# The second token group's last down pair as seven-of-eight rounds, mixed into the third group's first gate products, and half of the third group's y in a pool of its own

## The chip, the cores and the metric

The kernel runs on one core of one Trainium2 chip. The metric is the time of one execution in device microseconds (us); lower is better. Before the change it is 1999.62 us, the median of three runs (1998.15 to 1999.84).

## The reference, cut to what matters

The reference is one decoder layer on 2048 prompt tokens and 8 sample tokens (2056 in all), with a width of 1024 and a feed-forward width of 2816, in fp32. The change touches the last stage only:

```python
D_MODEL = 1024
D_FF = -(-8 * D_MODEL // (3 * 256)) * 256          # 2816
...
h = x + jnp.einsum('bte,ed->btd', mix, w_out)
hn = _rmsnorm(h, norm2_g)
ff = jax.nn.silu(jnp.einsum('btd,df->btf', hn, w_gate)) * jnp.einsum('btd,df->btf', hn, w_up)
y = h + jnp.einsum('btf,fd->btd', ff, w_down)
...
y_prompt = _rmsnorm(yp, final_norm_g)
y_sample = _rmsnorm(ys, final_norm_g)
```

What comes ahead of it (input projection, a gated linear recurrence, sliding-window attention, output projection) is the same work before and after.

## The kernel before, in words

**Products.** An fp32 product is made of three matmuls in fp32r: high part of the weight by high part of the data, high by low, and low by high. A high part is a cast on ACT; the low part is what the cast left over, a subtraction on DVE or POOL.

**Groups, pairs and products.** The feed-forward stage goes over three groups of tokens (`HALVES`: twice 344, twice 342 and twice 342 tokens; I call them the first, second and third group, 0, 1 and 2 in names). Inside a group it goes over 11 pairs (`NPAIR`) of 128-wide blocks of the feed-forward width. The gate and the up product of a pair are seven block products in place of eight each (a Strassen-Winograd scheme; `PRODS` is their order: 1, 2, 6, 5, 7, 3, 4), each of 12 matmuls of 128x342. A matmul is named after its product: g2_0_1 is gate product 1 of the third group's pair 0, u1_10_4 is up product 4 of the second group's pair 10. Their data are the hn tiles (the normed h, with sums and differences of its blocks).

**Down.** The pair's gated product then goes through w_down into y, 16 tiles of 128 x 342 (8 row tiles m, two token halves n) that hold h at first. There are two forms. The direct one (`down`, PSUM tiles pd) takes 16 tiles x 2 blocks x 3 = 96 matmuls and 16 adds into y on DVE. The seven-of-eight form (`down_parts`, PSUM tiles pw) takes 14 rounds of 2 tiles x 3 = 84 matmuls and 28 adds. A round n is product `DPRODS[n % 7]` of half `n // 7`. The data of its seven products are called T: four of them lie in the tiles fh and fl (high and low parts, one buffer for each), three (6, 7 and 4) in the t tiles, t2_0 and t2_1 for the third group. `wino(gi, p)` chooses: before, the direct form is used for pairs 0 to 2 of the first group and for the last pair of every group, the other for the rest. The rounds of pair p are mixed into the products of pair p+1. The direct down of a group's last pair runs behind the first three gate products (`N_EARLY`) of the next group.

**Weights of the rounds.** `down_make` (first group that uses a pair's rounds) loads w_down in pieces (rd), makes their sums on DVE and POOL, splits them into high and low parts (wd: ACT cast L1972, POOL or DVE low part L1973) and stores the sums to a buffer in DRAM, sums_d. `down_load` (later groups) loads the sums from there.

**Rooms.** One pool, bigp, has 16 buffers of three slots each. It holds the hn of the first three products, y (16 slots, 6 buffers for a group) and the t tiles (2 buffers). A new tile takes the room that the order gives it, and its first write waits until the last use of what was there before has ended. y is loaded from DRAM (`y_load`).

**Finish.** When y of a token half is complete, `finish` squares and adds it (DVE and POOL), sums over partitions on PE (st_f), makes the inverse root, transposes it to a row on PE (tr_f), copies the row out (ACT L1149), stores it to DRAM (rows_f, L1150) and loads it again as a tile with the row in every partition (rb_f, L1156), scales the eight y tiles on DVE (L2195) and stores them (out_yT, L2196). f1_1 is the finish of the second group's token half 1. The stores and loads are issued from one queue, SP's.

**Order.** `plan()` gives every product, round and finish a planned time. From these come priorities, and the order of instructions on each engine is written out in a long table, `ORDER`, which is recorded as dependencies: no engine departs from it.

Of the kernel before, what the change touches and what calls it, by code (L numbers as in the profile page):

```python
# [2383 lines left out]
```

## Time and profile before

| | |
|---|---|
| time, median of 3 runs | 1999.62 us (1998.15 to 1999.84) |
| the profiled execution | 1999.11 us, of which the profile's span is 1997.0 |
| mean granted clock of TensorE | 0.997 of full speed |
| PE (matmul) busy | 1971.0 us, 99% of the span |
| PEld (weight load) busy | 1874.8 us, 94% |
| DVE busy | 1560.6 us, 78% |
| ACT busy | 981.3 us, 49% |
| POOL busy | 959.8 us, 48% |
| moved by DMA | 461.93 MB, 231 GB/s over the span |

Busy time is the time in which an engine worked, summed over its instructions. Matmuls overlap their neighbours, so that a busy PE may still lose time by small steps. The second group's last pair and the third group's first pairs run between about 1500 and 1620 us of the span.

### The profile page before, as it was taken

The page shows a single profiled execution, that of the slowest core. Times are in us where ns is not written, and L with a number is a line of the kernel's source. Part 1 is how long each engine was busy: PE and PEld are TensorE (multiplying, and loading weights), DVE is VectorE, ACT ScalarE, POOL GpSimd, SP SyncE. Part 2 cuts the span into 40 slices and gives each one's busy share as a digit, 9 for nine tenths or more (in the row PEclk, how much of TensorE's full clock was granted, in tenths as well). Part 3 has the DMA queues.
Part 4 walks back from the last instruction along what each step waited for, and adds up shares of the span by engine and source line. Part 5 has one row for each costly group of instructions (what it writes and reads, how often), then busy time and mean ns, then how long its engine had stood idle before and what let it go on. Part 6 is the DMA issues. An engine that isn't in the chain of part 4 may idle for free. (4 is left out here: it accounts for less than half of the span.)

```text
span 1997.0 us, 34846 instructions
## 1 busy us (share of the span) xinstructions
PE 1971.0 (99%) x12112; PEld 1874.8 (94%) x12112; DVE 1560.6 (78%) x2894; ACT 981.3 (49%) x2032; POOL 959.8 (48%) x821
## 2 busy tenths in 40 slices
PE   8999999999999999999999999999999999999998
PEld 8988898888877999999999999999999999999998
DVE  7887986777986888888998786886668586766776
ACT  6775774664664534444446433433345433433433
POOL 5412362130233896788998754534456423322323
PEclk9999999999999999999999999999999999999999
DMA  8873586576688978655667886776558675565552
GB/s 314 287 252 138 194 300 198 183 254 210 223 283 291 335 263 268 220 215 210 246 241 279 265 289 231 234 237 210 191 191 267 228 259 199 179 211 195 180 181 103
DMA packets 218470, 461.93 MB, mean 231 GB/s; under 512 B 26230, under 2 KB 90406, under 8 KB 218278
## 3 DMA queue, kind: packets, MB, share of 16 engines
q1 hardware_dynamic: 214662, 456.69, 67.4%
q10 hardware_dynamic: 3632, 3.02, 0.4%
q8 instruction: 95, 1.56, 0.3%
q14 instruction: 81, 0.66, 0.1%
HBM read 345.51 MB, written 115.17 MB: 231 GB/s over the span
## 5 line engine op out<-in xcount | busy, mean ns | idle before, releaser
L1070 PE MATMUL ps_g<-hn,w_g 128*128 128x342 f32 (+1 forms) x2772 | 569.4, 320 | 0.3 <-DMA w_g<-split_g 0.3
L1070 PE MATMUL ps_u<-hn,w_u 128*128 128x342 f32 (+1 forms) x2772 | 559.5, 320 | 1.5 <-DMA w_u<-split_u 0.9
L1070 PEld LDWEIGHTS ps_g<-hn,w_g 128*128 128x128 f32 x2772 | 461.3, 188 | 1.2 <-ACT wd L1972 0.5
L1070 PEld LDWEIGHTS ps_u<-hn,w_u 128*128 128x128 f32 x2772 | 459.5, 188 | 3.0 <-ACT c_u L2115 1.6
L2175 DVE TENSOR_TENSOR y<-y,pw 128x342 f32<-128x342 f32 (+1 forms) x756 | 359.1, 504 | 114.7 <-PE pw L1070 108.4
L1070 PE MATMUL ip<-xn,w_in 128*128 128x512 f32 (+1 forms) x1680 | 365.2, 357 | 6.1 <-ACT xn L1105 5.7
L1070 PEld LDWEIGHTS ip<-xn,w_in 128*128 128x128 f32 x1680 | 269.6, 189 | 45.8 <-ACT xn L1105 5.7
L1070 PE MATMUL pw<-fh,wd 128*128 128x342 f32 (+1 forms) x864 | 253.4, 320 | 0.5 <-DVE y L2175 0.5
L1070 PE MATMUL pw<-t,wd 128*128 128x342 f32 (+1 forms) x972 | 243.7, 320 | 2.8 <-DVE y L2175 2.7
L1070 PE MATMUL op<-mix,w_out 128*128 128x512 f32 (+1 forms) x960 | 205.8, 355 | 0.4 <-ACT mix L1544 0.4
L1070 PEld LDWEIGHTS op<-mix,w_out 128*128 128x128 f32 x960 | 157.5, 189 | 25.3 <-ACT mix L1544 0.8
L1070 PEld LDWEIGHTS pw<-t,wd 128*128 128x128 f32 x972 | 169.9, 188 | 4.9 <-DVE y L2175 4.0
L1973 POOL TENSOR_TENSOR wd<-rd,wd 128x512 fp32r<-128x512 f32 x85 | 121.8, 1434 | 103.4 <-ACT wd L1972 99.1
L1972 ACT CAST wd<-rd 128x512 fp32r<-128x512 f32 x159 | 98.6, 621 | 130.0 <-PE ps_u L1070 39.8
L1070 PEld LDWEIGHTS pw<-fh,wd 128*128 128x128 f32 x864 | 158.6, 188 | 1.2 <-DVE y L2175 0.8
L1904 POOL TENSOR_TENSOR w_u<-ru,w_u 128x512 fp32r<-128x512 f32 x44 | 61.4, 1395 | 170.2 <-ACT w_u L1903 95.9
L1070 PE MATMUL pw<-fl,wd 128*128 128x342 f32 (+1 forms) x432 | 132.9, 320 | 0.0
L2089 DVE TENSOR_TENSOR c_u<-c_u,ps_u 128x342 f32<-128x342 f32 (+1 forms) x99 | 50.2, 508 | 101.2 <-PE ps_u L1070 93.9
L2071 POOL TENSOR_TENSOR c_u<-c_u,c_g 128x342 f32<-128x342 f32 (+1 forms) x60 | 65.4, 1090 | 124.8 <-DVE c_u L2089 115.1
L2060 DVE TENSOR_TENSOR fl<-c_u,fh 128x342 fp32r<-128x342 f32 (+1 forms) x132 | 105.4, 803 | 17.7 <-ACT fh L2059 17.0
L2059 ACT CAST fh<-c_u 128x342 fp32r<-128x342 f32 (+1 forms) x132 | 63.0, 480 | 110.6 <-POOL c_u L2071 49.3
L1070 PE MATMUL pd<-fh,w_d 128*128 128x344 f32 (+1 forms) x384 | 92.9, 320 | 0.0
(319 smaller groups left out, 3490.7 us busy)
## 6 DMA issues: line engine op xcount, KB each, us to landing
w_g<-split_g SPq DMA_DIRECT2D x88, 512.0 KB
w_u<-split_u SPq DMA_DIRECT2D x88, 512.0 KB
w_in<-split_w SPq DMA_DIRECT2D x84, 512.0 KB
rg<-in_wgate SPq DMA_DIRECT2D x110, 256.0 KB
ru<-in_wup SPq DMA_DIRECT2D x110, 256.0 KB
w_out<-split_w SPq DMA_DIRECT2D x48, 512.0 KB
split_g<-w_g SPq DMA_DIRECT2D x44, 512.0 KB
split_u<-w_u SPq DMA_DIRECT2D x44, 512.0 KB
```

The lines of the kernel that those rows point to most:

```text
L1070: r = nc.tensor.matmul(*args, **kw)
L1904: lo_eng.tensor_tensor(w[:, 1, :], src, w[:, 0, :].bitcast(F32), op=ALU.subtract)
L1972: nc.scalar.copy(w[:, :, 0], v)
L1973: eng((E_DLO0, E_DLO1, E_DLO2)[gi][j]).tensor_tensor(w[:, :, 1], v, w[:, :, 0].bitcast(F32), op=ALU.subtract)
L2059: nc.scalar.copy(hi, v)
L2060: nc.vector.tensor_tensor(lo, v, hi.bitcast(F32), ALU.subtract)
L2071: (nc.vector if p == NPAIR - 1 or src is not v else eng(E_MUL[2 * h + n])).tensor_tensor(v, src, g, op=ALU.mult)
L2089: nc.vector.tensor_tensor(o, a, b, op)
L2175: nc.vector.tensor_tensor(v, v, ps, ALU.add)
```

## The change: what it does

The second group's last pair takes the seven-of-eight form, and its 14 rounds stand behind the third group's first gate products. Eight of the 16 y tiles of the third group (row tiles 0, 1, 4 and 5 of both token halves) are loaded into a new pool, yx, that nothing else uses; the other eight stay in bigp, where they now take 3 buffers in place of 6. The sums of a pair's down weights are stored to sums_d only where the next group will load them (`wino(gi + 1, p)`). The order table is written anew for all engines.

```diff
 def wino(gi, p):
-    return p < NPAIR - 1 and (gi > 0 or p >= 3)
+    return gi == 1 or p < NPAIR - 1 and (gi > 0 or p >= 3)
...
-            mixed = p and wino(gi, p - 1)
+            gq, q = (gi, p - 1) if p else (gi - 1, NPAIR - 1)
+            mixed = gq >= 0 and wino(gq, q)
...
-                prod[gi, p, "gu"[i // 7], i % 7] = t - (U_D if gi and not p and i < N_EARLY else 0)
+                prod[gi, p, "gu"[i // 7], i % 7] = t - (U_D if gi and not p and not mixed and i < N_EARLY else 0)
                 t += U_M
-                if mixed and i >= (R_AT if p > 1 else R_FIRST):
+                if mixed and i >= (R_AT if p != 1 else R_FIRST):
                     for n in range(n, min(14, n + 2)):
-                        rounds[gi, p - 1, n] = t
+                        rounds[gq, q, n] = t
                         t += U_R
                     n += 1
+        if wino(gi, p):
+            end.append(t + R_AT * U_M + 7 * (U_M + 2 * U_R))
+            continue
...
+            yx = B(tc.tile_pool(name="yx", bufs=1))
...
-                        y = ys[gi, n, m] = next(place)[:, :nn]
+                        if gi == 2 and m % 4 < 2:
+                            y = yx.tile([P, TP], F32, tag=f"y{n}{m}", name=f"yx_{n}{m}")[:, :nn]
+                        else:
+                            y = next(place)[:, :nn]
+                        ys[gi, n, m] = y
...
-                    if j not in (3, 6):
+                    if j not in (3, 6) and wino(gi + 1, p):
...
                                 nc.vector.tensor_tensor(v, v, ps, ALU.add)
+                        if p == NPAIR - 1 and r in (2, 3, 4, 7):
+                            fire(("y", gi) + {2: (0, m), 3: (1, m), 7: (1, m + 4), 4: (0, m + 4)}[r])
...
     "PE": """
...
-ip0_1_0 ip0_1_1 ip0_1_0 ip0_1_1 ip0_1_0 ip0_1_1 w_st_x0:2 ip0_1_0 w_st_x0:2 ip0_1_1 w_st_x0:3 ip0_12_0:2 ip0_1_0:2
+ip0_1_0 ip0_1_1:2 ip0_1_0:2 ip0_1_1 w_st_x0 ip0_12_1 ip0_12_0 ip0_12_1 w_st_x0 ip0_12_0 ip0_12_1 ip0_12_0 ip0_1_0
```

In numbers of instructions: direct down matmuls 192 before and 96 after, round matmuls 1680 and 1764; DVE adds from pd into y 32 and 16, from pw into y 560 and 588 (140 of them into yx); loads of down weights of 128 KB 134 and 144, of 256 KB 24 and 20.

In the rows below a name ends in a number that the build gives it; what stands ahead of that is group, pair, product and, for pw, the tile (pw1_10_5_1 is product 5, tile 1 of the second group's pair 10). First PE, at the group boundary, behind the last matmuls of u1_10_4. Before:

```order
L1070 MATMUL ps_u1_10_1_17738<-hn1_1_10_13085,w_u1_10_4_17795 128x342
L1070 MATMUL ps_g2_0_2_18028<-hn2_0_3_17849,w_g2_0_2_17853 128x342
L1070 MATMUL ps_g2_0_2_18028<-hn2_0_4_17859,w_g2_0_2_17853 128x342 x4
L1070 MATMUL ps_g2_0_2_18028<-hn2_0_5_17877,w_g2_0_2_17853 128x342
L1070 MATMUL ps_g2_0_1_17995<-hn2_0_6_17891,w_g2_0_6_17889 128x342 x3
L1070 MATMUL ps_g2_0_2_18028<-hn2_0_4_17859,w_g2_0_2_17853 128x342
L1070 MATMUL ps_g2_0_1_17995<-hn2_0_7_17895,w_g2_0_6_17889 128x342
L1070 MATMUL ps_g2_0_1_17995<-hn2_0_6_17891,w_g2_0_6_17889 128x342
L1070 MATMUL ps_g2_0_1_17995<-hn2_0_7_17895,w_g2_0_6_17889 128x342 x2
L1070 MATMUL pd1_10_1_1_18071<-fh1_10_01_7623,w_d1_10_00_17884 128x342
```

And after:

```order
L1079 MATMUL ps_u1_10_1_17807<-hn1_1_10_13088,w_u1_10_4_17906 128x342
L1079 MATMUL ps_g2_0_2_18049<-hn2_0_3_17692,w_g2_0_2_17945 128x342
L1079 MATMUL ps_g2_0_2_18049<-hn2_0_4_17715,w_g2_0_2_17945 128x342 x4
L1079 MATMUL ps_g2_0_2_18049<-hn2_0_5_17719,w_g2_0_2_17945 128x342
L1079 MATMUL ps_g2_0_1_18030<-hn2_0_6_17736,w_g2_0_6_17962 128x342 x3
L1079 MATMUL ps_g2_0_2_18049<-hn2_0_4_17715,w_g2_0_2_17945 128x342
L1079 MATMUL pw1_10_5_1_18103<-fh1_10_01_7626,wd1_10_0_17998 128x342
L1079 MATMUL ps_g2_0_1_18030<-hn2_0_7_17753,w_g2_0_6_17962 128x342
L1079 MATMUL ps_g2_0_1_18030<-hn2_0_6_17736,w_g2_0_6_17962 128x342
L1079 MATMUL pw1_10_1_0_18088<-fh1_10_00_7625,wd1_10_0_17998 128x342
```

Behind the last u1_10_4 matmul 14 gate matmuls came before the first direct one; now 10 come before the first round. Next PE around the transpose of the second group's finish, tr_f1_1, some 60 us later. Before, the next rows are gate products and rounds on fh2_0 and fl2_0, and the first matmul on t2_0 stands 69 rows behind (tr_f1_0, the other half's, 33 rows behind):

```order
L1070 MATMUL ps_g2_1_5_18540<-hn2_1_6_17987,w_g2_1_3_18465 128x342
L1075 MATMUL tr_f1_1_18557<-cs_104,cols_f1_1_18453 3x114
L1070 MATMUL ps_g2_1_5_18540<-hn2_1_6_17987,w_g2_1_3_18465 128x342 x3
L1070 MATMUL ps_g2_1_5_18540<-hn2_1_7_17991,w_g2_1_3_18465 128x342
L1070 MATMUL ps_g2_1_5_18540<-hn2_1_6_17987,w_g2_1_3_18465 128x342
L1070 MATMUL ps_g2_1_5_18540<-hn2_1_7_17991,w_g2_1_3_18465 128x342 x3
L1070 MATMUL pw2_0_5_1_18690<-fh2_0_01_7641,wd2_0_0_18527 128x342
L1070 MATMUL pw2_0_1_1_18680<-fh2_0_00_7640,wd2_0_0_18527 128x342
```

After:

```order
L1079 MATMUL ps_u2_1_5_18858<-hn2_1_2_17786,w_u2_1_5_18698 128x342 x3
L1084 MATMUL tr_f1_1_18782<-cs_104,cols_f1_1_18683 3x114
L1079 MATMUL pw2_0_5_1_18655<-fh2_0_11_7646,wd2_0_1_18568 128x342
L1079 MATMUL pw2_0_5_1_18655<-fl2_0_11_7650,wd2_0_1_18568 128x342
L1079 MATMUL pw2_0_5_1_18655<-fh2_0_11_7646,wd2_0_1_18568 128x342
L1084 MATMUL tr_f1_0_18817<-cs_104,cols_f1_0_18711 3x114
L1079 MATMUL pw2_0_1_3_18853<-fh2_0_00_7643,wd2_0_3_18693 128x342
L1079 MATMUL pw2_0_1_3_18853<-fl2_0_00_7647,wd2_0_3_18693 128x342
L1079 MATMUL pw2_0_1_3_18853<-fh2_0_00_7643,wd2_0_3_18693 128x342
L1079 MATMUL pw2_0_1_0_18634<-t2_0_7655,wd2_0_1_18568 128x342
```

Both transposes now stand among the up products of pair 1, and the first matmul on t2_0 eight rows behind tr_f1_1. Last ACT, around its first write of t2_0, with what each row waits for (DMAHW with a digit is the semaphore of one DMA queue, the others those of engines). Before:

```order
L1972 CAST wd2_0_1_18624<-rd2_0_1_18530 128x2x256 [waits DMAHW7_49,PE_49,Activation_49]
L2059 CAST t2_0_7652<-c_u2_0_01_7649 128x342 [waits DVE_49]
L2059 CAST t2_0_7652<-c_u2_0_11_7651 128x342 [waits Pool_49]
L2115 COPY c_g2_1_01_7655<-ps_g2_1_1_18469 128x342 [waits PE_49]
L1903 CAST w_u2_1_2_18629<-ru2_1_01_18535 128x512 [waits DMAHW5_49,DMAHW0_49]
```

After:

```order
L1158 COPY row_f1_1_18784<-tr_f1_1_18782 3x114 [waits PE_49]
L1158 COPY row_f1_0_18819<-tr_f1_0_18817 3x114 [waits PE_49]
L1917 CAST w_g2_2_1_18898<-rg2_2_00_18805 128x512 [waits DMAHW3_49,DMAHW1_49]
L2073 CAST t2_0_7655<-c_u2_0_11_7654 128x342 [waits DMAHW6_49,DVE_49]
L2073 CAST t2_0_7655<-c_u2_0_01_7652 128x342
L2073 CAST t2_1_7656<-c_u2_0_10_7653 128x342 [waits DMAHW2_49,DMAHW0_49,DMAHW7_49,DVE_49,Pool_49]
L2129 COPY c_u2_1_01_7670<-ps_u2_1_1_18666 128x342 [waits DVE_49]
L2131 COPY c_u2_1_11_7672<-ps_u2_1_5_18858 128x342 [waits DVE_49]
```

The casts into t2_0 and t2_1 stand behind the copies of the finish's rows, and they have waits on DMA queues that they did not have. Those are stores of the second group's y: in bigp, t2_0 comes into the room of y1_5 and t2_1 into that of y1_1, where before they came into those of an hn tile and of a t tile of the second group; y2_0, y2_1 and y2_2 come into the rooms of t1_0, t1_1 and y1_0.

More of the change, by code (lines that the diff above doesn't have):

```diff
@@ L441 @@
-u2_0_4:6 st_f1_1 g2_1_6 u2_0_4 st_f1_1 u2_0_4 g2_1_6:3 st_f1_1 g2_1_2 g2_1_6 g2_1_2 g2_1_6 g2_1_2:9 g2_1_6:2 g2_1_2
-g2_1_6:3 st_f1_0:3 g2_1_5 g2_1_6 g2_1_5:10 g2_1_7 w2_0_1_0 w2_0_5_0 g2_1_5 g2_1_7:11 g2_1_3:4 tr_f1_1 g2_1_3:8
-w2_0_5_1 w2_0_1_1:2 w2_0_5_1 w2_0_1_0 w2_0_1_1 w2_0_5_0:2 w2_0_5_1 w2_0_1_0 u2_1_1 g2_1_4:3 u2_1_1:11 g2_1_4:9
-u2_1_2:11 tr_f1_0 u2_1_2 u2_1_6:12 w2_0_2_0:3 u2_1_7:11 u2_1_5:12 u2_1_7 u2_1_3:12 u2_1_4:7 g2_2_1 u2_1_4 g2_2_1
-u2_1_4:4 w2_0_6_1:3 w2_0_6_0:3 g2_2_1:7 w2_0_1_3:2 g2_2_2 w2_0_1_3 g2_2_1:2 g2_2_2 g2_2_1 g2_2_2:9 w2_0_7_0:3 g2_2_2
@@ new lines @@
+g2_1_6:2 g2_1_2 g2_1_6:3 st_f1_0:3 g2_1_5 g2_1_6 g2_1_5:10 g2_1_7 w2_0_5_0 g2_1_5 g2_1_7:11 g2_1_3:12 w2_0_5_1
+w2_0_1_1 w2_0_5_1 w2_0_1_0 w2_0_1_1 w2_0_5_0:2 w2_0_5_1 w2_0_1_0 u2_1_1 g2_1_4:3 u2_1_1:11 g2_1_4:9 u2_1_2:12
+u2_1_6:12 w2_0_2_0:3 w2_0_3_0:3 u2_1_5:12 tr_f1_1 w2_0_3_1:3 tr_f1_0 w2_0_1_3:3 w2_0_6_0 w2_0_6_1 w2_0_6_0 w2_0_6_1:2
+g2_2_1:2 w2_0_6_0 g2_2_1:7 w2_0_6_3:3 w2_0_7_0 g2_2_1:3 w2_0_7_0:2 u2_1_7:12 w2_0_4_0:3 w2_0_7_1:3 u2_1_4:12
+w2_0_2_1:3 w2_0_1_2:2 w2_0_7_3:2 w2_0_4_1:3 w2_0_1_2 w2_0_7_3 w2_0_5_2:3 u2_1_3:12 w2_0_2_2:3 g2_2_2:12 w2_0_5_3:3
@@ new lines @@
+g2_6_1 u2_5_3 u2_5_7 g2_6_1:2 u2_5_3 u2_5_7 u2_5_3:5 g2_6_1 u2_5_3:3 w2_5_1_0 u2_5_3 w2_5_1_0:2 u2_5_3 u2_5_4
+w2_5_1_1:3 u2_5_4:7 g2_6_6 u2_5_4 g2_6_6 u2_5_4 g2_6_6 u2_5_4:2 g2_6_6 g2_6_2 g2_6_6 g2_6_2:6 g2_6_6:2 g2_6_2:5
+g2_6_6:3 w2_5_5_1 g2_6_6:2 w2_5_5_0 g2_6_5 w2_5_5_0 g2_6_5 w2_5_5_1 g2_6_5:3 w2_5_5_0 g2_6_5 w2_5_5_1 g2_6_5:3
+w2_5_6_0 g2_6_5 w2_5_6_0 g2_6_5:2 w2_5_6_1:2 w2_5_6_0 w2_5_6_1 w2_5_2_0:2 g2_6_7:2 w2_5_3_1 g2_6_7:3 w2_5_2_0
+w2_5_3_0:3 g2_6_7:3 w2_5_3_1:2 g2_6_7:4 w2_5_7_0:2 w2_5_7_1:3 g2_6_3:3 w2_5_7_0 g2_6_3:2 w2_5_2_1:2 g2_6_3 w2_5_2_1
@@ new lines @@
+wd2.0 f10 pu2.0 wd2.0 wu2.1 pu2.1:2 wd2.0 pu2.1 wd2.1 pu2.1 wg2.2 pu2.1 wd2.1:2 wu2.2 pu2.2:2 wd2.2 pu2.2:3 wd2.2
+wg2.3 wd2.2 wu2.3 pu2.3:2 wd2.3 pu2.3:3 wd2.3 wg2.4 wd2.3 wu2.4 pu2.4:2 wd2.4 pu2.4:3 wd2.4 wg2.5 wd2.4 wu2.5 pu2.5:2
+wd2.5 pu2.5:3 wd2.5 wg2.6 wd2.5 wu2.6 pu2.6:4 wd2.6 pu2.6 wd2.6 wg2.7 wd2.6 wu2.7 pu2.7:2 wd2.7 pu2.7:3 wd2.7 wg2.8
+wd2.7 wu2.8 pu2.8:2 wd2.8 pu2.8:3 wd2.8 wg2.9 wd2.8 wu2.9 pu2.9:2 wd2.9 pu2.9:3 wd2.9 wg2.10 wd2.9 wd2.10 wu2.10
+wd2.10 wd2.10+1 wd2.10 f21:2 f20 f21 f20:3 f21 f20:2
@@ L851 @@
[L851 removed]
+wd2.7:4 wu2.7:3 wg2.8+4 wu2.8 wg2.8 wd2.7 wg2.8 wd2.7 wg2.8 wu2.8 wg2.8 wd2.7 wg2.9 wu2.8+4 wd2.8 wg2.9 wd2.8 wu2.8
+wd2.8 wd2.8+1 wu2.8 wd2.8 wu2.8:2 wg2.9+4 wu2.9 wd2.8 wg2.9:2 wd2.8 wg2.9 wu2.9 wg2.9 wd2.8 wg2.10 wu2.9+4 wd2.9
+wg2.10 wd2.9:2 wu2.9 wd2.9:2 wu2.9:3 wg2.10+4 wu2.10 wg2.10:2 wd2.9:2 wg2.10 wu2.10 wg2.10 wd2.9 wd2.10 wu2.10+4
+wd2.10:2 wu2.10:3 wd2.10 wu2.10 f21:2 f21+1 f21:2 f21+1 f21+1 f21 f20:4
 """,
```

1171 lines of the change are left out of this document (581 added, 590 removed).

## The prediction, made before the changed kernel ran

> **What bounds the kernel now.** I read the page first, then the stretches of 50 us, then the chain of waits, and last the instructions in order of time around the change.
>
> ```profile
> PE 1971.0 (99%) x12112; PEld 1874.8 (94%) x12112; DVE 1560.6 (78%) x2894; ACT 981.3 (49%) x2032; POOL 959.8 (48%) x821
> 1500.00:1550.00 50.00, 50.00 (x320) 50.00 (x319) 40.99 (x69) 29.49 (x68) 34.59 (x31) 1.00 0.82 273
> 1550.00:1600.00 50.00, 48.20 (x307) 46.92 (x305) 28.59 (x49) 19.99 (x43) 20.03 (x18) 1.00 0.69 232
> 1600.00:1650.00 50.00, 49.56 (x313) 49.01 (x313) 40.67 (x85) 16.52 (x34) 11.12 (x10) 1.00 0.78 259
> 1650.00:1700.00 50.00, 50.00 (x320) 50.00 (x319) 36.85 (x68) 21.13 (x44) 19.33 (x17) 1.00 0.54 186
> 1536.39 8.81 PE pd L1070 x56
> ```
>
> TensorE is the bound: 99% of the span, and its share is full in the stretch where the change begins (second and third row; the columns after the length are PE, PEld, DVE, ACT and POOL busy, the clock, the DMA share and GB/s). The last row is a piece of the chain of waits: 56 matmuls in 8.81 us, so one more or less costs 8.81 / 56 = 0.157 us. The 0.32 us that one lasts overlap its neighbours. Behind the group boundary PE is not full: 1.80 + 0.44 us idle in 1550 to 1650. The waits there:
>
> ```profile
> 1593.65 3.26 PE L1070 MATMUL ps_u<-hn,w_u 128*128 128x342 f32 x19 [0.44 <-ACT c_u L2117]
> 1599.26 0.74 PE L1070 MATMUL pw<-t,wd 128*128 128x342 f32 x3 [1.24 <-DVE y L2175]
> 1600.16 0.73 PE L1070 MATMUL pw<-t,wd 128*128 128x342 f32 x3 [0.16 <-DVE y L2175]
> 1612.87 1.17 PE L1070 MATMUL ps_g<-hn,w_g 128*128 128x342 f32 x6 [0.28 <-DMA w_g<-split_g]
> ```
>
> They come from the second group's finish, whose scalings fill the DVE and whose stores fill the SP queue.
>
> **Fewer matmuls.** The pair's 96 direct matmuls (2 token halves, 8 row tiles, 2 blocks, 3 parts) become 14 rounds of 2 x 3 = 84. 12 x 0.157 = -1.9 us, all on the path, since PE is full on either side.
>
> **Rounds packed close.** From the last product of u1_10 on, 48 of the next 64 matmuls belong to rounds (8 rounds of 6), so up to there the DVE sets whether PE can follow. Prices, and where that stretch begins:
>
> ```profile
> L2175 DVE TENSOR_TENSOR y<-y,pw 128x342 f32<-128x342 f32 (+1 forms) x756 | 359.1, 504 | 114.7 <-PE pw L1070 108.4
> L2060 DVE TENSOR_TENSOR fl<-c_u,fh 128x342 fp32r<-128x342 f32 (+1 forms) x132 | 105.4, 803 | 17.7 <-ACT fh L2059 17.0
> L1973 POOL TENSOR_TENSOR wd<-rd,wd 128x512 fp32r<-128x512 f32 x85 | 121.8, 1434 | 103.4 <-ACT wd L1972 99.1
> L1972 ACT CAST wd<-rd 128x512 fp32r<-128x512 f32 x159 | 98.6, 621 | 130.0 <-PE ps_u L1070 39.8
> 1527.93 0.31 PE L1070 MATMUL ps_u<-hn,w_u 128*128 128x342 f32 x1
> 1528.28 0.52 DVE L2071 TENSOR_TENSOR c_u<-ps_u,c_g 128x342 f32<-128x342 f32 x1 [0.99 <-PE ps_u L1070]
> 1530.00 1.23 DVE L2060 TENSOR_TENSOR fl<-c_u,fh 128x342 fp32r<-128x342 f32 x1
> 1604.01 6.79 DVE L2175 TENSOR_TENSOR y<-y,pw 128x342 f32<-128x342 f32 x15
> 1613.05 0.70 DVE L1973 TENSOR_TENSOR wd<-rd,wd 128x512 fp32r<-128x512 f32 x1
> ```
>
> The DVE takes the last u product at 1528.28; PE's last matmul of it began 0.35 earlier, at 1527.93. From there to the add that frees the bank of round 4 (matmul 62, 1527.93 + 62 x 0.157 = 1537.7) the DVE's new order holds a product and an add (0.5 each), five low parts (0.80 each), one split of a down weight (0.70) and 11 adds at 6.79 / 15 = 0.45: 1.0 + 4.0 + 0.7 + 5.0 = 10.7 us, to 1539.0. PE loses 1539.0 - 1537.7 = +1.3 us. With every low part at 1.23 it is 3.4; with every one at 0.5, as a PSUM add, nothing (an earlier start of PE is not possible): 0 to 3.4. In "SBUF — State Buffer" (section "Who interferes with whom") the Trainium skill says that a DVE instruction with two SBUF inputs contends with a GpSimd instruction that reads SBUF, and that one with a single SBUF input does not. The rows agree (803 against 504), and as POOL works without a break there, that page would put the low parts at the 1.23 row and this term at 3.4.
>
> The new splits and sums of weights (ACT 0.6 each, POOL 1.4, by the third and fourth row) lie beside PE. They delay POOL's last low part of the third group's hn, but the six squares' sums that stood ahead of it now come behind, so I add nothing; the upper end below holds 1.5 us for it. Ten weight loads of 128 KB, in place of four of 256 KB, stand in the SP queue between hn loads; the eight loads into yx stand behind the last of these. At a DMA share of 0.82 there are gaps left, and they cost nothing unless hn comes late, which the same 1.5 covers.
>
> **The new wait.** The third group's t tiles no longer follow the second group's t tiles in their room: y2_0 and y2_1 now get that room, and t2_0 follows y1_5, t2_1 follows y1_1. These are y of the second group, and are free only when finish has scaled and stored them. ACT's write of t2_0 waits for the store of y1_5, behind the scaling, the broadcast row, the row's store and the transpose tr_f1_1 on PE; and tr_f1_1 now stands only six round matmuls (and one more transpose) ahead of the first matmul that reads t2_0. The same chain before, with cover enough:
>
> ```profile
> 1577.86 0.26 PE L1075 MATMUL tr_f<-cs,cols_f 114*3 114x114 f32 x1
> 1578.15 0.24 ACT L1149 COPY row_f<-tr_f 3x114 f32<-3x114 f32 x1 [1.10 <-PE tr_f L1075]
> 1578.42 0.26 SPq L1150 DMA_DIRECT2D rows_f<-row_f  x1
> 1579.87 0.32 SPq L1156 DMA_DIRECT2D rb_f<-rows_f  x1
> 1583.15 2.03 DVE L2195 SCALAR_TENSOR_TENSOR y<-y,vec,rb_f 128x342 f32<-128x342 f32 x4 [0.77 <-DMA rb_f<-rows_f]
> 1130.90 0.24 PE L1075 MATMUL tr_f<-cs,cols_f 86*4 86x86 f32 x1
> 1136.86 3.68 DVE L2195 SCALAR_TENSOR_TENSOR y<-y,vec,rb_f 128x344 f32<-128x344 f32 x5 [0.94 <-DMA rb_f<-rows_f]
> 1137.47 0.34 SPq L2196 DMA_DIRECT2D out_yT<-y  x1
> 1594.19 3.07 DMA out_yT<-y
> 1146.27 5.04 DMA out_yT<-y
> 1151.74 2.73 DMA y<-hs
> 1576.57 0.48 ACT L2059 CAST t<-c_u 128x342 fp32r<-128x342 f32 x1
> ```
>
> From tr to the first scaling: 1583.15 - 1577.86 = 5.3 us (5.96 in the first group). From the scaling to its store's issue 0.6 (1137.47 - 1136.86). The store 3.07 (5.04 in the other row; 2.73 for a load of the same size). ACT's cast 0.5. In all 5.3 + 0.6 + 3.1 + 0.5 = 9.5, and PE has 6 x 0.157 and a transpose, 1.1 us, to do. PE idles +8.4 us, since its order is fixed and all behind stays behind. Ends: 5.3 + 0.6 + 2.7 + 0.5 - 1.1 = 8.0 and 5.96 + 0.6 + 5.04 + 0.5 - 1.1 = 11.0; I take 8.4, from the rows of the same group.
>
> Next is t2_1, which waits for three stores of y1_1. The last of them follows the eighth scaling, 8 x 0.5 behind the start of the first, so t2_1 is free some 3.4 us after t2_0; PE has 22 matmuls (3.5 us) up to the one that reads it. The cast and the low part behind it (0.5 + 0.5) stay: +1.0, between 0 and 2. u2_1_3's weights are queued on SP behind 13 of these stores, but 46 matmuls (7.2 us) are left by then: nothing. Who waits for SP there otherwise (w_g2_2_6, the last y loads) has more.
>
> **The clock.** Where PE idled in the input stage:
>
> ```profile
> 219.93 0.47 PE L1070 MATMUL bc_at<-cs,atcols 104*128 104x104 f32 x2 [2.35 <-ACT rb_at L1140]
> 220.00:221.00 1.00, 1.00 (x6) 0.87 (x7) 0.50 (x2) 0.57 (x2) 0.00 (x0) 1.00 0.17 70
> 221.00:222.00 1.00, 1.00 (x5) 0.82 (x4) 1.00 (x2) 0.71 (x2) 0.00 (x0) 0.72 0.00 0
> 222.00:223.00 1.00, 1.00 (x4) 0.81 (x4) 1.00 (x3) 1.00 (x3) 0.00 (x0) 0.50 0.00 0
> 223.00:224.00 1.00, 1.00 (x5) 0.81 (x4) 0.42 (x1) 1.00 (x3) 0.75 (x1) 0.50 0.00 0
> 224.00:226.00 2.00, 2.00 (x12) 1.82 (x11) 1.82 (x2) 0.72 (x2) 1.95 (x3) 0.78 0.14 35
> ```
>
> After 2.35 us without a matmul the granted clock falls to 0.50, and 0.28 + 0.50 + 0.50 + 2 x 0.22 = 1.7 us of full speed are lost. A wait of 8.4 us is longer, so +1.7, between 0 (a lucky place of the drop inside the wait) and 2.5 (one more half-speed stretch at the second wait). "TensorE: Matmul & The Clock Gate" (section "What's actually happening") in the Trainium skill halves the clock only after an idle window of about 3.4 us. The trace differs: 2.35 us were enough. By that page the term stays for one wait of 8.4, but falls away, with a sum of 1.7 less, if the wait comes in pieces below 3.4.
>
> **What goes.** The four waits above (0.44 + 1.24 + 0.16 + 0.28 = 2.1 us) end in the time that PE now stands still: -2.1, between -2.1 and 0. The eight yx tiles are loaded long before their first add.
>
> **The sum.** -1.9 + 1.3 + 8.4 + 1.0 + 1.7 - 2.1 = +8.4 us. The profiled execution took 1999.11 us for a span of 1997.0; with the 8.4 it is 2007.5. That execution lies 0.5 below the median 1999.62, within the runs shown (1998.15 to 1999.84), so I leave it at 2007.5. Lower ends: -1.9 + 0 + 8.0 + 0 + 0 - 2.1 = +4.0, 2003.1. Upper: -1.9 + 3.4 + 1.5 + 11.0 + 2.0 + 2.5 = +18.5, 2017.6; not all at once.
>
> **Rivals.** About 0.2%, 4 us, is what a measurement of this kernel tells from no change.
> *Faster: the chain is over in time.* Place: the first matmul on t2_0. It decides at 1.1 us from tr_f1_1 to the cast; then the new wait, its second part and the clock cost nothing, and the packed rounds are hidden too: -1.9 - 2.1 = -4.0, 1995.1. For it: those waits did come from the finish, and half of y is now out of its way. Against: the shortest such chain quoted takes 5.3 us to the scaling alone. 0.05.
> *No change: the chain is short.* With an emptier SP queue and DMA rings (0.69 there), the two row transfers might need half of their 1.45 + 3.28 us, a store 2.0, and the drop in clock is missed: 2.9 + 0.6 + 2.0 + 0.5 - 1.1 = 4.9; 4.9 + 1.3 - 4.0 = +2.2, 2001.3. Against: no row shows such transfers. 0.10.
> *Slower still: the packed rounds are paced by DVE and POOL together*, each low part at 1.23, hn 1.5 late, a store of 5.04 behind other loads: +3.4 + 1.5 + 11.0 + 1.0 + 1.7 - 1.9 - 2.1 = +14.6, 2013.7. For it: that 1.23 row; against: fl's mean of 803. 0.10.
> My forecast has the remaining 0.75.
>
> **Numbers.** Faster 0.05, the same 0.11, slower 0.84 (the forecast, the last rival, less a little for the forecast's own tail below 2003.6). The range goes from 2001.5, just above the no-change case, to 2014, which holds the last rival's centre.
>
> **What would show it.** In the changed kernel's profile: PE without an idle row up to some 10 us behind the last u1_10 matmul, then 1 to 3 us lost among pw rows with DVE y as the releaser; some 60 us behind it a tr_f row, and 1 us later one idle row of 8 us on PE at pw<-t, released by ACT t, which itself waited for DMA out_yT<-y; a clock near 0.5 right behind it; then PE full again. The mechanism is wrong if that idle row is under 3 us; the sum is wrong if the packed rounds lose over 4 us, or if waits show at ps_g of the third group's first pair for hn or weights.

## The result: 2012.47 us, slower by 0.68%, and the profile after

The changed kernel takes 2012.47 us (median of 4 runs, 2011.97 to 2013.73) against 1998.88 beside it; the ratio is 1.0068, with a 95% interval of 1.0055 to 1.0080. The forecast was 2007.5, 5.0 us less. The profiled execution took 2013.73 us for a span of 2011.9, at a mean clock of 0.992 (0.997 before).

The page's row of busy times, and the stretches of 50 us that were shown of before:

```profile
PE 1978.9 (98%) x12100; PEld 1881.6 (94%) x12100; DVE 1577.4 (78%) x2913; ACT 982.5 (49%) x2038; POOL 971.6 (48%) x832
1500.00:1550.00 50.00, 49.02 (x307) 47.87 (x306) 40.77 (x74) 28.16 (x64) 36.74 (x33) 1.00 0.74 249
1550.00:1600.00 50.00, 48.43 (x309) 47.32 (x308) 34.92 (x55) 22.96 (x51) 29.86 (x27) 1.00 0.72 248
1600.00:1650.00 50.00, 43.33 (x255) 42.25 (x255) 40.80 (x85) 15.87 (x33) 11.31 (x10) 0.90 0.67 223
```

There are 12 fewer matmuls, and yet PE is busy 7.9 us longer: matmuls at half clock last longer. (The counts of direct and round matmuls given with the change are those of the 342-token tiles alone; the difference of 12 is the same over all tiles.) The stretch 1600 to 1650 holds 255 of them in place of 313, with PE idle for 6.7 us and a mean clock of 0.90. PE's waits there, in order of time (L1079 is the matmul helper, L2073 and L2074 the cast and low part of T, L2189 an add into y, L1987 the low part of a down weight, L1158 the row copy; one more, of 0.19 us for c_g, stands at 1558.78):

```profile
1538.65 0.57 PE L1079 MATMUL pw<-fh,wd 128*128 128x342 f32 x2 [0.50 <-DVE y L2189]
1540.47 0.74 PE L1079 MATMUL pw<-t,wd 128*128 128x342 f32 x3 [0.47 <-POOL wd L1987]
1596.53 2.13 PE L1079 MATMUL ps_u<-hn,w_u 128*128 128x342 f32 x12 [1.05 <-DMA w_u<-split_u]
1599.78 0.43 PE L1079 MATMUL pw<-fh,wd 128*128 128x342 f32 x1 [0.33 <-ACT row_f L1158]
1606.45 0.94 PE L1079 MATMUL pw<-t,wd 128*128 128x342 f32 x2 [5.94 <-ACT t L2073]
1608.13 1.23 PE L1079 MATMUL pw<-t,wd 128*128 128x342 f32 x3 [0.74 <-DVE t L2074]
```

The four waits of before are gone. The one that was forecast is there: 5.94 us at the first matmul on t2_0. The chain behind it, followed through the queues (the first row is another thing: the load for which PE waited at 1596.53; the last two are the low part of t2_0 and the cast into t2_1):

```profile
1590.83 0.32 SPq L1941 DMA_DIRECT2D w_u<-split_u  x1
1598.50 0.26 PE L1084 MATMUL tr_f<-cs,cols_f 114*3 114x114 f32 x1
1598.80 0.24 ACT L1158 COPY row_f<-tr_f 3x114 f32<-3x114 f32 x1 [3.08 <-PE tr_f L1084]
1599.07 0.92 SPq L1159 DMA_DIRECT2D rows_f<-row_f  x2
1600.21 1.01 SPq L1165 DMA_DIRECT2D rb_f<-rows_f  x2
1603.19 4.46 DVE L2211 SCALAR_TENSOR_TENSOR y<-y,vec,rb_f 128x342 f32<-128x342 f32 x9 [1.74 <-DMA rb_f<-rows_f]
1603.80 6.51 SPq L2212 DMA_DIRECT2D out_yT<-y  x9
1605.92 0.86 ACT L2073 CAST t<-c_u 128x342 fp32r<-128x342 f32 x2 [5.68 <-DMA out_yT<-y]
1607.57 0.51 DVE L2074 TENSOR_TENSOR t<-c_u,t 128x342 fp32r<-128x342 f32 x1
1609.19 0.48 ACT L2073 CAST t<-c_u 128x342 fp32r<-128x342 f32 x1 [2.41 <-DMA out_yT<-y]
```

From the transpose to the first scaling 4.69 us, to its store's issue 0.61, to the end of the store 2.12, to the matmul 0.53. The cast's own wait names the store of y. PE's next wait, 0.74, is for the low part at 1607.57. The cast into t2_1 comes only at 1609.19, so this is t2_0's own low part, which stood behind nine scalings on DVE; for t2_1 PE has no idle row. And the clock around it (the fifth number from the left is DVE's, the third from the right the granted clock):

```profile
1603.00:1606.40 3.40, 0.00 (x0) 0.00 (x0) 3.21 (x7) 0.48 (x2) 0.00 (x0) 0.53 0.34 117
1606.40:1610.00 3.60, 2.81 (x8) 2.25 (x9) 3.50 (x8) 0.86 (x2) 0.88 (x1) 0.50 0.67 243
1610.00:1613.40 3.40, 3.40 (x13) 3.40 (x13) 3.10 (x7) 0.70 (x2) 0.24 (x1) 0.50 0.83 292
1613.40:1616.00 2.60, 2.60 (x18) 2.60 (x18) 1.13 (x3) 0.64 (x2) 0.00 (x0) 0.99 0.81 212
```

Half speed lasts from 1603.2 to 1613.4, 10.2 us. The first 3.2 lie inside the wait and cost nothing more; in the other 7.0, less the wait of 0.74, half of the work is lost: 3.1 us.

Where the time went is read from the start of the same matmul in both profiles:

| first matmul of | before | after | shift |
|---|---|---|---|
| g0_0_1 | 650.0 | 654.6 | +4.6 |
| g1_2_1 | 1162.1 | 1167.5 | +5.4 |
| g2_0_1 (ahead of all that the change moves) | 1519.0 | 1524.4 | +5.5 |
| u2_1_1 | 1580.8 | 1586.9 | +6.1 |
| g2_2_1 | 1596.8 | 1609.2 | +12.4 |
| u2_2_1 | 1631.8 | 1646.3 | +14.5 |
| end | 1997.0 | 2011.9 | +15.0 |

The row of g2_2_1 is not like for like: from g2_0_1 to there PE has 464 matmuls after and 493 before, 12 of the 29 by the change and 17 (2.7 us) because the new order puts them behind it. In the other rows the counts are equal up to g2_0_1, and 12 or 13 lower behind it.

So two parts: +9.5 us behind g2_0_1 (forecast +8.4), and +5.5 ahead of it, which the prediction did not have. In the early part there are three waits near 300 us that before does not have (1.69 us together, two are shown), and a lower clock near 603 and 1160. But other waits are gone: from 20 us to g2_0_1 PE's idle rows add up to 9.0 us after and 8.7 before. The half speed weighs more: four periods of 3.413 us ahead of g2_0_1 for one before, and three of them cost up to 5.1 us. After:

```profile
295.91 0.68 PE L1079 MATMUL st_h<-avg,hacc 128*104 128x1 f32 x6 [1.08 <-ACT row_x L1158]
307.09 0.33 PE L1084 MATMUL pt<-cs,sc 128*128 128x128 f32 x1 [0.43 <-DVE ptl L1670]
601.28 0.63 PE L1084 MATMUL pt<-cs,sc 128*128 128x128 f32 x4 [0.84 <-DVE ptl L1670]
602.72 1.57 PE L1079 MATMUL st_h<-avg,hacc 128*128 128x1 f32 x8 [0.58 <-POOL hacc L1126]
600.00:610.00 10.00, 8.58 (x30) 6.92 (x31) 7.39 (x14) 4.18 (x8) 2.50 (x2) 0.66 0.70 208
```

And before, at the same place:

```profile
599.18 0.63 PE L1075 MATMUL pt<-cs,sc 128*128 128x128 f32 x4 [0.81 <-DVE ptl L1661]
600.62 1.05 PE L1070 MATMUL st_h<-avg,hacc 128*128 128x1 f32 x8 [0.57 <-POOL hacc L1117]
600.00:610.00 10.00, 9.07 (x46) 7.10 (x46) 8.59 (x15) 7.13 (x15) 1.78 (x2) 1.00 0.60 189
```

The same two short waits (near 600) stand in both; the clock fell behind them in one execution and not in the other.

### The profile page after: what moved, and what is told of

Read it like the earlier page. It is cut to its first block, busy times and chain, and to the rows that moved or that the text cites. A ratio compares the mean times of both kernels' runs of the same rounds, so it can differ in the third digit from the quotient of the medians.

```text
span 2011.9 us, 34874 instructions
## 1 busy us (share of the span) xinstructions
PE 1978.9 (98%) x12100; PEld 1881.6 (94%) x12100; DVE 1577.4 (78%) x2913; ACT 982.5 (49%) x2038; POOL 971.6 (48%) x832
## 4 chain that ended last, share of the span: by engine, by line
PE 91%; DVE 4%; DMA 2%; ACT 1%; issue 1%; POOL 1%; SPq 0%; DVEq 0%; ACTq 0%; POOLq 0%
PE ps_g L1079 21%; PE ps_u L1079 21%; PE pw L1079 18%; PE ip L1079 14%; PE op L1079 7%; PE pd L1079 4%; PE s L1079 1%; PE o L1079 1%; PE pt L1084 1%; PE g L1079 1%; DMA hn<-mixed 0%; DVE xc L1466 0%; ACT sc L1655 0%; DMA w_u<-split_u 0%; DMA rb_x<-rows_x 0%
## 5 line engine op out<-in xcount | busy, mean ns | idle before, releaser
L1079 PE MATMUL ps_g<-hn,w_g 128*128 128x342 f32 (+1 forms) x2772 | 569.7, 320 | 0.0
L1079 PE MATMUL ps_u<-hn,w_u 128*128 128x342 f32 (+1 forms) x2772 | 557.9, 319 | 1.9 <-DMA w_u<-split_u 1.7
L1079 PEld LDWEIGHTS ps_g<-hn,w_g 128*128 128x128 f32 x2772 | 462.4, 189 | 0.5
L1079 PEld LDWEIGHTS ps_u<-hn,w_u 128*128 128x128 f32 x2772 | 459.2, 188 | 2.9 <-ACT wd L1986 1.7
L2189 DVE TENSOR_TENSOR y<-y,pw 128x342 f32<-128x342 f32 (+1 forms) x644 | 306.2, 504 | 100.1 <-PE pw L1079 95.0
L1079 PE MATMUL ip<-xn,w_in 128*128 128x512 f32 (+1 forms) x1680 | 367.9, 359 | 7.1 <-ACT xn L1114 5.7
L1079 PEld LDWEIGHTS ip<-xn,w_in 128*128 128x128 f32 x1680 | 272.2, 191 | 47.3 <-ACT xn L1114 5.7
L1079 PE MATMUL pw<-fh,wd 128*128 128x342 f32 (+1 forms) x896 | 264.6, 321 | 2.5 <-DVE wd L1987 1.2
L1079 PE MATMUL pw<-t,wd 128*128 128x342 f32 (+1 forms) x1008 | 254.6, 323 | 7.8 <-ACT t L2073 5.9
L1079 PE MATMUL op<-mix,w_out 128*128 128x512 f32 (+1 forms) x960 | 206.4, 356 | 0.8 <-DVE xr L1443 0.8
L1079 PEld LDWEIGHTS pw<-t,wd 128*128 128x128 f32 x1008 | 177.8, 191 | 10.5 <-ACT t L2073 6.2
L1079 PEld LDWEIGHTS op<-mix,w_out 128*128 128x128 f32 x960 | 157.9, 190 | 25.6 <-issue 1.1
L1987 POOL TENSOR_TENSOR wd<-rd,wd 128x512 fp32r<-128x512 f32 x87 | 123.3, 1419 | 95.4 <-ACT wd L1986 90.9
L1079 PEld LDWEIGHTS pw<-fh,wd 128*128 128x128 f32 x896 | 165.1, 189 | 4.2 <-DVE y L2189 1.5
L1079 PE MATMUL pw<-fl,wd 128*128 128x342 f32 (+1 forms) x448 | 137.9, 321 | 0.0
L2073 ACT CAST fh<-c_u 128x342 fp32r<-128x342 f32 (+1 forms) x132 | 63.0, 479 | 117.3 <-POOL c_u L2085 46.1
L2074 DVE TENSOR_TENSOR fl<-c_u,fh 128x342 fp32r<-128x342 f32 (+1 forms) x132 | 105.2, 801 | 15.2 <-ACT fh L2073 14.4
L1917 ACT CAST w_u<-ru 128x512 fp32r<-128x512 f32 x99 | 61.4, 620 | 61.5 <-PE pw L1079 26.6
```

The source lines that it names most:

```text
L1079: r = nc.tensor.matmul(*args, **kw)
L1917: nc.scalar.copy(w[:, 0, :], src)
L1987: eng((E_DLO0, E_DLO1, E_DLO2)[gi][j]).tensor_tensor(w[:, :, 1], v, w[:, :, 0].bitcast(F32), op=ALU.subtract)
L2073: nc.scalar.copy(hi, v)
L2074: nc.vector.tensor_tensor(lo, v, hi.bitcast(F32), ALU.subtract)
L2189: nc.vector.tensor_tensor(v, v, ps, ALU.add)
```

## The experiments

All are edits of the changed kernel unless it is said otherwise; most edit the order table alone. Times are medians.

| label | us | ratio to before, 95% interval | end minus g2_0_1, against before |
|---|---|---|---|
| (the changed kernel) | 2012.47 | 1.0068, 1.0055 to 1.0080 | +9.5 |
| early_before | 2011.29 | 1.0060, 1.0047 to 1.0072 | +10.7 |
| early2 | 2008.33 | 1.0046, 1.0034 to 1.0059 | +9.8 |
| before_early_after | 2008.87 | 1.0045, 1.0032 to 1.0058 | +4.2 |
| finish_early | 2008.50 | 1.0045, 1.0031 to 1.0059 | +5.9 |
| finish_w | 2007.94 | 1.0044, 1.0032 to 1.0057 | +9.1 |
| both_w | 2005.24 | 1.0038, 1.0024 to 1.0051 | +9.8 |
| both_w2 | 2004.99 | 1.0036, 1.0023 to 1.0049 | +6.3 |
| rooms | 2006.00 | 1.0037, 1.0023 to 1.0051 | +5.9 |
| rooms2 | 2001.68 | 1.0019, 1.0010 to 1.0028 | +2.1 |
| rooms3 | 2002.17 | 1.0014, 1.0006 to 1.0023 | +3.9 |
| fill_wait | 2015.03 | 1.0075, 1.0062 to 1.0088 | +11.7 |
| zero_fill | 2012.50 | 1.0062, 1.0049 to 1.0075 | +6.6 |

The last column comes from the one profiled execution of each. None beats the kernel before (1998.22 to 1999.71 beside these runs).

**The early part: early_before, early2, before_early_after.** The order table of one kernel up to a place, of the other from there on: up to the group boundary (early_before), up to 1350 us (early2), and the reverse on the kernel before (before_early_after).

In words, since the edit is the long table itself:

```diff
-ORDER, every engine, up to the place: as in the changed kernel
+ORDER, every engine, up to the place: as in the kernel before
```

> The changed kernel with the order of before up to the group boundary (about 1500 us), on all engines; from there on as changed. In the two profiles the changed kernel reaches the third group 5.5 us later, before any matmul of the change has run: 2.2 us by waits, the rest by two drops of the clock near 603 and 1160 us. Theory (the new order ahead of the boundary costs it): 2012.5 - 5.5 = 2007, no clock drop at 603. First rival (only its waits are the order's, the clock drops are chance): 2010.3. Second rival (all of it is chance of the profiled execution): 2012.5.

> The changed kernel with the order of before up to 1350 us on all engines, where both orders read alike for at least 49 instructions ahead and 56 behind on each, so that there is no seam as in early_before (waits of 0.65 + 1.64 there). Theory (the new order ahead of the boundary costs its waits, 2.2 us near 300; what the clock loses near 603 comes with either order, by chance): 2012.5 - 2.2 = 2010.3. Rival (the early order costs nothing): 2012.5. Second rival (it costs the clock too): 2007.

> The kernel before with the changed kernel's order up to the group boundary, and its own behind it. Theory (that order costs by itself): 1998.9 + 5.5 = 2004.4. First rival (its waits alone): 2001.1. Second rival (chance): 1998.9.

early_before came out between the expectations, with waits of its own at the seam by the boundary (1.6 us at one). early2 has no seam: 2008.33, 4.1 below the changed kernel. In the reverse, before gets slower by 0.45%, more than any theory had, with a wait of 2.75 us at the seam. The start of g2_0_1 says the same over more executions: with the changed kernel's early order it was +5.5, +3.3, 0.0, +7.7, +5.2 and +5.2 us against before (mean 4.5, six profiles), with before's early order 0, +1.8, +2.2, -3.6, -0.8, +1.3, -1.5 and +2.2 (mean 0.2, eight). So some 4 us go with the order of instructions ahead of the change, which is the same work. The profiles show of what they consist. Periods of 3.413 us at half speed ahead of g2_0_1: 16 in the six profiles and 9 in the eight, 2.7 and 1.1 each, a difference of 2.6 us at most. PE's idle rows from 20 us to there: 10.2 and 8.1 us each, 2.1 more. Two waits stand in all six and in none of the eight, 1.06 to 1.08 us near 295 and 0.46 to 0.47 near 1052. So the waits come with the order; how many of the drops do stays open, since single executions of one order have 0 to 2 or 1 to 4 of these periods.

**The chain alone: finish_early.** One plan time of the finish is changed for the second group, so that both transposes, row copies, rows, scalings and stores stand 13.5 us earlier; the rooms are the same.

```diff
-yield t + dt * (F_FIN[2] + F_FIN[3])
+yield t + dt * (F_FIN[2] + (3.5 if gi else F_FIN[3]))
...
-g2_1_3:12 w2_0_5_1
+g2_1_3:10 tr_f1_1 g2_1_3:2 w2_0_5_1
```

> The changed kernel with the second group's transposes tr_f1_1 and tr_f1_0, the row copies, row transfers, scalings and stores of its finish 13.5 us earlier in the orders of PE, ACT, SP and DVE; rooms as in the changed kernel. Theory (t2_0 waits for y1_5's store only because the finish stands late): the waits of 5.94 + 0.74 + 0.33 and the half-speed stretch of 10.24 us (5.1 lost) go: 2012.5 - 12.1 = 2000.4. Rival (the scalings then collide with the adds of the rounds on DVE and with the weight loads on SP, and the wait moves there): 2006 or more, with waits at pw for DVE y. Second rival (the room is not what is waited for): 2012.5.

2008.50, 4.0 below the changed kernel, where the theory asked for 12.1 and the rival for 6.5 at most: the rival's number holds, and its wait for a weight load; the waits for adds that it named do not show here. The wait at the first matmul on t2_0 is gone (1.04 us for its low part are left), and another stands where the room of a weight comes free late and its load now queues behind two of the stores:

```profile
1590.96 0.82 SPq L2206 DMA_DIRECT2D out_yT<-y  x2
1591.83 0.80 SPq L1935 DMA_DIRECT2D w_u<-split_u  x1
1598.40 3.76 PE L1073 MATMUL ps_u<-hn,w_u 128*128 128x342 f32 x12 [4.90 <-DMA w_u<-split_u]
```

**The next ones in the queue: finish_w, both_w, both_w2.** finish_w adds to finish_early the load of w_u2_1_5 right behind rb_f, its 12 matmuls behind six round matmuls, and the casts of t2_0 earlier. both_w is that with before's early order (as in early2). both_w2 puts 25 DVE instructions of both_w in another order, two adds ahead of the scalings and one behind eight of them.

```diff
-u2_1_5:12 w2_0_3_1:3 w2_0_1_3:3
+w2_0_3_1:3 w2_0_1_3:3 u2_1_5:12
```

> As finish_early (2008.5), and on SP the load of w_u2_1_5 goes straight behind the finish's broadcast rows, ahead of the y stores, with w_u2_1_6 and four yx loads earlier too; on PE the 12 matmuls of u2_1_5 stand behind six round matmuls that were behind them; ACT's casts into t2_0 and DVE's first low part stand ahead of the split of w_g2_2_1. Theory (in finish_early PE waits 4.9 us for w_u2_1_5, whose load was issued behind two stores, and loses 3.4 by the clock for that): 2008.5 - 4.9 - 3.4 = 2000.2, between 1999 and 2003. Rival (the stores and loads fill the DMA there, whatever the order, and one of them is late): a wait for another load or store of 3 us or more, 2005 or more.

> finish_w and early2 together: the order of before up to 1350 us, the change with an early finish behind it. Theory: finish_w - 2.2 = 1998, that is 0.5 to 1 below before (12 matmuls fewer, 1.9, and 2.1 of waits gone, against some 1 for the packed rounds and 1 to 2 of new waits). Rival (the seven-of-eight rounds are no gain even without the wait): 2001 or more.

> both_w (2005.2) with another order on DVE alone, in 25 instructions around the finish of the second group: the adds of pw2_0_1_0 and pw2_0_5_1 stand ahead of the scalings (in both_w DVE waited 5.5 us for the broadcast row and then did 11 scalings in 6.4 us ahead of them, and PE waited 6.3 for the bank of pw2_0_2_0), that of pw2_0_2_0 behind eight scalings, then t2_0's low part and c_u2_1_00 ahead of the rest. Theory (the change gains its 12 matmuls and the old waits once neither the room, nor the weight load, nor DVE's order holds PE): 2005.2 - 6.3 - 5.1 (three half-speed stretches) - 1 to 2 of the last wait = 1993 to 1995, and below before. Rival (another wait of 3 us or more comes up in its place): 1999 to 2004.

Each missed its theory. The rivals of the first two have the right numbers (2005 or more, 2001 or more), but not the right reason: the wait is no load's, and it is still there. In finish_w PE waits for a PSUM bank, whose add stands behind eleven scalings:

```profile
1588.39 6.44 DVE L2205 SCALAR_TENSOR_TENSOR y<-y,vec,rb_f 128x342 f32<-128x342 f32 x11 [5.27 <-DMA rb_f<-rows_f]
1594.75 0.50 DVE L2183 TENSOR_TENSOR yx<-yx,pw 128x342 f32<-128x342 f32 x1
1596.21 0.65 PE L1073 MATMUL pw<-fh,wd 128*128 128x342 f32 x1 [6.04 <-DVE yx L2183]
```

both_w has the same wait (6.30), and both_w2 3.18 there, behind eight scalings; that is the wait of its rival, at a time 1 us above the rival's range. The scalings could not simply stand back: the t tiles needed the rooms that they free. both_w against finish_w, 2.7 us less by the medians, fits the early order again, though the intervals of the two overlap.

**The rooms: rooms, rooms2, rooms3.** The room of a tile goes by the order in which the tiles are first written. In these three, y is loaded in two passes, so that t2_0 is written ahead of y2_1 and gets the second group's t1_1's room, free some 40 us earlier or more (the last matmul on a t tile of the second group stands at 1556.8 in rooms, the store of y1_5 ends at 1598.2); t2_1 gets y1_5's (one store), y2_1 that of y1_1. Then the casts of t2_0 stand ahead of the finish's scalings. The rest is as in both_w2.

```diff
-for m in range(KD):
-    yield t + m
+for m in (0, 1, 2, 4, 5, 3, 6, 7) if gi == 2 else range(KD):
+    yield (t + m,) + ((("T", 2, 0, 7),) if gi == 2 and m in (3, 6, 7) else ())
```

> The version with before's early order, the earlier finish and the reordered adds (2004.99 us), and now the rooms changed: the third group's t2_0 takes the room of the second group's t1_1 (free long before), t2_1 that of y1_5 (one store only), and y2_1 that of y1_1; the casts of t2_0 and its low part therefore stand ahead of the finish's scalings, two adds (of the rounds with tiles pw2_0_1_0 and pw2_0_2_0) behind the first three of them, and both row loads rb_f ahead of three yx loads. Theory (what is left of the loss is the wait of the t tiles and of the adds behind the scalings that the t tiles made urgent): the four waits of 3.18, 0.28, 0.99 and 1.17 us near 1595 go, and with them the 6.83 us at half speed, of which at least half is saved: 2004.99 - 5.6 - 1.7 = 1997.7, range 1996 to 2000.5. Rival (the finish itself, 16 scalings on DVE and 16 stores on SP beside 28 adds, sets the pace whatever rooms it frees): the wait comes back at another bank or weight, 2003 or more.

No wait for t is left: the first five matmuls on t2_0 follow the u product without a gap, and ACT casts into t2_0 at 1583.59 without a wait for a store, where in both_w2 it waited for one until 1596.30. But 2006.00, the rival's side, as an add and a product (c_u) that PE needs stood behind scalings:

```profile
1594.58 0.95 PE L1072 MATMUL pw<-t,wd 128*128 128x342 f32 x5
1599.62 0.42 PE L1072 MATMUL pw<-t,wd 128*128 128x342 f32 x1 [1.60 <-DVE yx L2182]
1607.18 3.42 PE L1072 MATMUL ps_u<-hn,w_u 128*128 128x342 f32 x12 [3.53 <-DVE c_u L2096]
```

rooms2 and rooms3 differ from it in the DVE's order alone (and rooms3 in one load's place): first c_u2_1_11 and four adds between the scalings, then five adds and a split ahead of the last seven.

> The version with the rooms changed (2006.00 us), and 25 instructions of the DVE put in another order: the product c_u2_1_11 and four adds from ahead of which all the finish's scalings stood now come between these, the add that freed the bank of pw2_0_1_0 (PE waited 1.60 for it) comes ahead of t2_1's low part. Theory (the two waits that are left there, 1.60 and 3.53 us, come only from adds standing behind scalings, and the half speed behind the longer one from that wait): 2006.0 - 5.1 - 1.5 = 1999.4, range 1998 to 2001.5, no different from before. Rival (the finish itself sets the pace; the wait comes back at another bank or weight): 2003 or more.

> The last version (2001.68 us), where PE still waited 2.43 and 1.05 us near 1603 for two adds behind scalings that lasted up to 1.24 us: the five adds into yx and y2_1 and one split that PE needs next now come ahead of the last seven scalings, and w_g2_2_6's load ahead of the last four stores. Theory (only adds behind scalings are left there; with them gone the boundary costs no more than the fewer matmuls save): 2001.68 - 3.5 - 0.3 = 1997.9, range 1996.5 to 2000.5, level with before or a little below. Rival (the finish still sets the pace, the wait comes back at a later bank or weight): 2001 or more.

rooms2 took 2001.68, just above the theory's range: 4.3 below rooms, 10.8 below the changed kernel (of which some 4 go with the early order). PE waits 2.43 and 1.05 us for adds. rooms3 did not go on (2002.17, by the ratio no different from rooms2): the waits came back some 6 us later, counted from g2_0_1. The DVE is full up to the first of them; ahead of the add of the second it stood still for 2.00 us, for a load of y, and those issued there stand behind four stores in SP's queue:

```profile
1600.00:1612.00 12.00, 11.48 (x74) 11.18 (x72) 11.26 (x24) 2.65 (x6) 2.62 (x2) 1.00 0.76 232
1612.68 0.42 PE L1072 MATMUL pw<-fh,wd 128*128 128x342 f32 x1 [1.20 <-DVE yx L2182]
1615.84 0.51 DVE L2182 TENSOR_TENSOR y<-y,pw 128x342 f32<-128x342 f32 x1 [2.00 <-DMA y<-hs]
1616.40 0.43 PE L1072 MATMUL pw<-fh,wd 128*128 128x342 f32 x1 [1.73 <-DVE y L2182]
```

DVE is busy for 11.26 of the 12 us up to 1612. So the larger wait of rooms3 is again one for a load behind the finish's stores, and not for a busy DVE. That the sixteen scalings and stores beside the adds of 14 rounds are what is left of the loss fits these rows, but no run shows it, as no version without the loss was found.

**The clock: fill_wait, zero_fill.** Matmuls that change nothing fill the wait: 46 on ones ahead of the last round before it (fill_wait), or 40 with zero weights behind that round (zero_fill).

```diff
+if (gi, p, r, m) == (2, 0, 1, 3):
+    for _ in range(40):
+        mm("z", ps[:, :256], zero_r, hi[:, :256], start=False, stop=True, skip_group_check=True)
```

> The changed kernel with 46 extra matmuls of 128x256 on ones (0.118 us each, 5.4 in all) between tr_f1_0 and the matmuls that follow, into a PSUM tile that is then overwritten; the wait for t2_0 stays as it is. Theory (the 10.24 us at half clock come from PE standing still): no half-speed stretch near 1604, 2012.5 - 5.1 = 2007.4, up to 0.5 more where the fills outlast the wait. Rival (the clock falls there whatever PE does): 2012.5 to 2013.

> The changed kernel with 40 extra matmuls of 128x256 with a weight of zeros (0.118 us each, 4.7 in all) ahead of the first matmul on t2_0, added into an open PSUM sum behind its first add on DVE, so that they fill the wait and nothing else waits for them (in fill_wait the extra matmuls stood ahead of that add, and the scalings behind it came later). Theory (the 10.24 us at half clock come from PE standing still): at most one drop of 3.41 there, 2012.5 - 3.4 to - 5.1 = 2007.4 to 2009.1. Rival (the clock does not depend on it): 2012.5.

fill_wait is confounded: the add of the delayed round stands ahead of the scalings on DVE, so the chain itself began later, and 3.58 us of wait and 6.83 at half speed were left. In zero_fill the clock stayed full:

```profile
1603.55 4.98 PE L1076 MATMUL pw<-fh,zero 128*128 128x256 f32 x40 [0.99 <-DVE y L2186]
1610.13 0.73 PE L1076 MATMUL pw<-t,wd 128*128 128x342 f32 x3 [1.15 <-DVE t L2071]
1606.40:1610.00 3.60, 2.57 (x21) 2.22 (x19) 3.60 (x9) 0.86 (x2) 0.00 (x0) 1.00 0.54 195
```

Its profile loses 2.8 us less behind g2_0_1 than the changed kernel's (+6.6 for +9.5), near the 3.1 worked out above. The median, 2012.50, is the rival's number and does not show it; that execution also started g2_0_1 2.2 us later, by 3.8 us more of waits and one period less at half speed ahead of it. So the clock's price at the wait is read from one profile, and not confirmed by the times.

## Why the prediction was right, and where it was short

| term | forecast | measured in the profile after |
|---|---|---|
| 12 fewer matmuls | -1.9 | 12100 for 12112; not priced again |
| rounds packed close | +1.3 | 0.50 (DVE) + 0.47 (POOL) = +1.0 |
| wait for t2_0 | +8.4 | 5.94, and 0.33 for the row copy ahead of it: +6.3 |
| second part (t2_1, low part) | +1.0 | +0.7, for t2_0's low part; t2_1 none |
| clock behind the wait | +1.7 | +3.1 |
| old waits gone | -2.1 | all four gone, -2.1 |
| weight w_u2_1_5 | nothing | +1.05 |
| c_g at 1558.78 | nothing | +0.2 |
| sum | +8.4 | +8.3 of +9.5 |

- **The mechanism** is shown from two sides: the cast's wait names the store, and in rooms, with t2_0 in another room, that wait does not exist (the cast comes 12.7 us earlier than in both_w2, from which rooms was made).
- **The wait was taken too long by 2.1 us.** Its chain took 7.95 us from tr_f1_1 to the matmul where 9.5 was the estimate: 4.69 for 5.3 to the scaling, 2.12 for 3.07 in the store. PE also had 0.9 us more to do or to wait for ahead of it (2.0 for 1.1).
- **The clock was taken too short**: 3.1 for 1.7, since half speed lasted for 10.2 us and not for 3.4. The upper bound was 2.5.
- **A wait that was costed at nothing**: PE stood 1.05 us for w_u2_1_5. Its load was issued at 1590.83, as soon as the last matmul that read its slot (begun at 1590.48) had ended, and the product could start 5.7 us later; the step on weights spoke of u2_1_3's only.
- **The packed rounds** lost near what was forecast, but only half of it, 0.50, at an add of DVE as the step says. Its five low parts took 0.59 to 1.23 us, 4.4 together where the 803 ns mean gave 4.0. The other 0.47 is a wait for POOL's split of a down weight, which the step had put beside PE, at nothing. By the Trainium skill's "SBUF — State Buffer" ("Who interferes with whom") the term was 3.4; the 0.97 measured here lies far below.
- **The second part** came near its size by another cause: t2_1 cost PE no idle row, and the 0.74 is t2_0's low part behind nine scalings, which the step did not have.
- **That the sum of the terms** (+8.4) comes so near the measured one (+8.3) is luck in part: -2.1 at the wait, +1.4 at the clock and +1.05 at the weight cancel. The total was 5.0 us short, and lies in the range because that reached up to 2014.
- Of the +9.5, 1.2 is not in any row. Part of it is how idle time is counted: a matmul lasts 0.32 us and the next begins 0.157 behind it, so each stop costs 0.16 more than its idle row. There are three more stops than before, 0.5 us. Another 0.5 lies between the first matmul of u2_10_4 and the end (32.5 us before, 33.0 after), far behind the change; over all profiles that piece takes 32.2 to 33.3. So little is left open.
- **The step that failed** is one that the prediction did not have: the order table was written anew for the whole program, and the working began at the group boundary. Ahead of it the profile shows +5.5, by up to 5.1 of it the clock, and the exchanges of order some 4 us. With these 4 the forecast would have stood at 2011.5.
- The rival "slower still" ended near the measured time (2013.7), but by other causes: the packed rounds lost 1.0 and not 3.4, the store took 2.12 and not 5.04, and no wait for hn shows.

## What to carry to other kernels

When a change gives a tile another room, ask what must have left that room, and price the whole chain up to that, also where it ends in a store; where rooms go by the order of first writes, a change of that order may be a cheaper cure than hurrying the chain. In a fixed order one wait that is taken away uncovers the next in the same queues: here the loss went from a room to a weight's load, to a PSUM bank whose add stood behind scalings, and in the last version to such an add and a load of y behind stores. No repair gave more than 4.3 us, where most were hoped to give 6 to 12. If the table of a whole program is written anew, compare the time at which the changed place is reached as well.
